# Scaling softmax probabilities on GpSimd in place of ScalarE in a hybrid encoder block

## The chip, the cores and the metric

The kernel runs on one core of a Trainium2 chip. The metric is the device time of one execution in microseconds (us); the median of the runs is compared. The engines of the core are TensorE (PE in the profile; its weight loads are shown apart as PEld), VectorE (DVE), ScalarE (ACT), GpSimd (POOL) and SyncE (SP), which issues nearly all DMAs. The TensorE clock that the throttle grants stands in the profile as a share of full speed.

## The reference

One layer of a bidirectional encoder block, for 1024 positions of width 1024, all in float32. A projection feeds two branches: gated linear attention (GLA) and attention in a window of +-128 positions (SWA). Their outputs are gated and projected, and a SwiGLU feed-forward follows. The change lies in the window attention: 8 query heads in two groups of 4, 2 key-value heads of width 128, blocks of 128 queries against up to three blocks of keys, and a learned sink logit that joins the softmax:

```python
scores = jnp.einsum("bnqhgd,bnkhd->bnhgqk", qb, kc) * (hd ** -0.5)
scores = jnp.where(mask[None, :, None, None], scores, -jnp.inf)
m = jnp.maximum(scores.max(axis=-1, keepdims=True), sink)
p = jnp.exp(scores - m)
denom = p.sum(axis=-1, keepdims=True) + jnp.exp(sink - m)
o = jnp.einsum("bnhgqk,bnkhd->bnqhgd", p / denom, vc)
```

## The kernel before

All products of float32 values are made from two parts: a value is rounded to a high part (on ScalarE, a copy to a reduced float32 format) and the rest is its low part (on VectorE, value minus high part), and three matmuls (line 76: high x high, high x low, low x high) make a product. Line 70 and line 72 do this for weights (wh, wl).

The program goes through the projections and the GLA branch, then from about 575 to 745 us through the window attention, then through the output projections, the gates and the feed-forward.

The window attention works on 16 blocks, 2 groups of heads x 8 blocks of 128 queries. Each block passes through stages in successive slots of a software pipeline (the list `todo`): its raw queries are loaded; a slot later they are normed and rotated (`a_prep`; the small tiles rt, rl and rs of lines 98 to 104 are the inverse norm, and qn the rotated queries); then transposed and split (`a_turn`: PE L923, ACT sqh L926, DVE sql L927); then scored (`a_scores`); two slots later the probabilities are transposed and split (`a_probs`) and multiplied by the values (`a_out`). So in one slot blocks n-2, n, n+1 and n+2 are worked on at once.

The steps of `a_scores` for a block: four heads one after another, three matmuls each into a PSUM buffer ch (line 76), and one VectorE instruction (line 941) that adds the band mask, writes the scores p to SBUF and their largest value mx. When all four are there, VectorE makes nm (the negated maximum, lines 948 to 950) and es (the sink's exponent, line 952); ScalarE exponentiates es (line 953) and the four heads of p (line 956, whose accumulator gives the row sum dn); VectorE adds es to dn (line 958) and takes the reciprocal rd (line 960); then the four heads of p are multiplied by rd (line 962). A row of p is 384 wide, or 256 at the two ends of the sequence.

In `a_probs`, for each of up to three key blocks, TensorE transposes the four heads (line 973) into ch; ScalarE makes the high part ph (line 976), VectorE the low part pl (line 977). In `a_out` TensorE makes three matmuls per key block, in the order ph x vSh, pl x vSh, ph x vSl (vSh and vSl are the parts of the values). ScalarE copies the output to sob (line 987), and four DMAs write it to DRAM. There are four PSUM buffers ch and four mm, and two buffers for p.

TensorE's order is written by hand: in a slot the steps come as a_probs, a_prep, a_scores, a_turn, a_out (with the key steps of the first blocks between), and between them stand matmuls of a dense projection, whose tiles are mm (15 matmuls a slot in most slots, 18 in the last ones). The order of the instructions on the other engines is chosen by a scheduler from its own cost estimates, so an edit of one instruction can reorder others. Each engine takes its instructions strictly in that order.

At the start of the slot in which the scores are over (three slots ahead of the end), `prep_b(0)` begins to load the finished outputs back from DRAM (lo) and to split them (obh on ScalarE, line 1001; obl on VectorE, line 1002) for the output projection. The gates of that projection (gb; VectorE line 1108, ScalarE line 1109) are loaded then too.

Of the kernel before, what the change touches and what calls it, by code (L numbers as in the profile page):

```python
# [11 lines left out]
AF = mybir.ActivationFunctionType  # L12
ALU = mybir.AluOpType
# [17 lines left out]
def body(tc, i, out):  # L31
    nc = tc.nc
    with ExitStack() as root:
# [8 lines left out]
        def nm(s):  # L42
            uid[0] += 1
            return f"{s}_{uid[0]}"
# [4 lines left out]
        def chtile(shape, dt=F32):  # L49
            return psc.tile(list(shape), dt, tag="ch", name=nm("ch"))  # L50
# [27 lines left out]
        def mm3(o, ah, al, bh, bl, start, stop):  # L78
            mm(o, ah, bh, start, False)
            mm(o, ah, bl, False, False)  # L80
            mm(o, al, bh, False, stop)
# [849 lines left out]
        def a_scores(g, n, h):  # L931
            a = att[g, n]
            if h == 0:
                a.p = sw.tile([P, 4, 384], F32, tag="p", name=nm("p"))
                a.mx = sw.tile([P, 4], F32, tag="mx", name=nm("mx"))
            w, p, mx = a.w, a.p, a.mx
            ks = slice(a.b0 * P, (a.b1 + 1) * P)
            mo = (a.b0 - (n - 1)) * P
            s = chtile((P, 384))
            mm3(s[:, :w], a.qh[:, h], a.ql[:, h], kTh[:, g, ks], kTl[:, g, ks], True, True)  # L940
            nc.vector.tensor_tensor_reduce(out=p[:, h, :w], in0=s[:, :w], in1=band[:, mo:mo + w],
                                           op0=ALU.add, op1=ALU.max, scale=1.0, scalar=-1e30,
                                           accum_out=mx[:, h:h + 1])
            if h < 3:
                return
            sk = sink[:, 4 * g:4 * g + 4]
            nm_ = sw.tile([P, 4], F32, tag="nm", name=nm("nm"))
            nc.vector.tensor_tensor(mx, mx, a.rs, op=ALU.mult)
            nc.vector.tensor_tensor(mx, mx, sk, op=ALU.max)
            nc.vector.tensor_scalar(nm_, mx, -1.0, None, op0=ALU.mult)  # L950
            es = sw.tile([P, 4], F32, tag="es", name=nm("es"))
            nc.vector.tensor_tensor(es, sk, mx, op=ALU.subtract)
            nc.scalar.activation(es, es, AF.Exp)
            dn = sw.tile([P, 4], F32, tag="dn", name=nm("dn"))
            for h in range(4):
                nc.scalar.activation(p[:, h, :w], p[:, h, :w], AF.Exp, bias=nm_[:, h:h + 1],  # L956
                                     scale=a.rs[:, h:h + 1], accum_out=dn[:, h:h + 1])
            nc.vector.tensor_tensor(dn, dn, es, op=ALU.add)
            rd = sw.tile([P, 4], F32, tag="rd", name=nm("rd"))
            nc.vector.reciprocal(rd, dn)  # L960
            for h in range(4):
                nc.scalar.activation(p[:, h, :w], p[:, h, :w], AF.Copy, scale=rd[:, h:h + 1])

        def a_probs(g, n, kb):
            a = att[g, n]
# [47 lines left out]
        for n in range(2 * KT):  # L1013
            g, t = divmod(n, KT)
            todo[n + 5].append((a_out, g, t))
            todo[n + 5] += [(a_probs, g, t, kb) for kb in range(3)]
            todo[n + 3] += [(a_scores, g, t, h) for h in range(4)]
            todo[n + 2].append((a_turn, g, t))
            todo[n + 1].append((a_prep, g, t))
            if n < KT:  # L1020
                todo[n + 1].append((k_turn, n))
                todo[n].append((k_prep, n))
                if n:
                    todo[n - 1].append((k_load, n))
            todo[n].append((a_load, g, t))
        order = (a_probs, k_prep, a_prep, a_scores, a_turn, k_turn, a_out, k_load, a_load)
        k_load(0)
        with tc.manual_schedule(engines={mybir.EngineType.PE}):
# [508 lines left out]
```

## Time and profile before

| | |
|---|---|
| median of 3 runs | 1648.97 us (1647.95 to 1650.07) |
| profiled execution | 1649.93 us |
| its span, first to last instruction | 1648.1 us |
| outside the span | 1.8 us |
| mean granted TensorE clock | 0.999 |
| busy: PE, DVE, ACT, POOL | 1628.2, 1249.4, 872.3, 0.2 us |

How to read it: the busy time of an engine is the time in which it executes, so its idle time is the span less that. A row of a timeline has the start (us), the duration (us), the engine, the line of the kernel, the operation, the tiles (out<-in, buffer numbers left out) and the shapes; in brackets at its end stand the idle time of the engine just ahead of it and what ended that. With x4 at its end a row stands for four instructions in a row. A row of the waits has the engine and tile that waited, what it waited for, then the us in total, the times, and the longest. A row of a window has its two ends, its length, the busy time and number of instructions on PE, PEld, DVE, ACT and POOL, the granted clock, the share of the DMA engines' time and GB/s. A row of a group of instructions has its busy time in us, the mean of one in ns, and the idle time ahead of them.

### The profile page before, as it was taken

The numbers are of one execution on the slowest core, as the hardware profiler recorded it, in microseconds if no ns is written. First come the engines' busy times: TensorE is split into PE (matmuls) and PEld (weight loads), VectorE is DVE, ScalarE is ACT, GpSimd is POOL, SyncE is SP. The second block draws the span as 40 slices with busy tenths as digits, with TensorE's granted clock in tenths as the row PEclk, the third lists the DMA queues.
The fourth block names the chain that finished last, engine by engine and source line by source line (L and its number), as shares of the span: only waits on it lengthen the run. The fifth ranks groups of instructions, "written<-read, shape, count | busy, mean of one in ns | idle before, by whom it ended". The sixth has DMA issues, their size and how long they took to land.

```text
span 1648.1 us, 23225 instructions
## 1 busy us (share of the span) xinstructions
PE 1628.2 (99%) x7588; PEld 1346.5 (82%) x7588; DVE 1249.4 (76%) x2559; ACT 872.3 (53%) x1826; POOL 0.2 (0%) x4
## 2 busy tenths in 40 slices
PE   9999999999999999999999999999999999999999
PEld 7888888888888778878888888888888888888887
DVE  8867665589986599857885678887777778779655
ACT  8622224468998688885554557333333333354442
POOL 0000000000000000000000000000000000000000
PEclk9999999999999999999999999999999999999999
DMA  7554334485554633238765554453334443496433
GB/s 235 171 184 147 116 118 138 170 253 173 178 162 128 190 115 97 74 124 280 226 205 171 168 152 148 128 160 109 103 109 155 146 147 128 168 349 192 147 98 120
DMA packets 168010, 262.90 MB, mean 160 GB/s; under 512 B 19325, under 2 KB 52861, under 8 KB 167889
## 3 DMA queue, kind: packets, MB, share of 16 engines
q1 hardware_dynamic: 167888, 261.42, 49.9%
q8 instruction: 60, 0.98, 0.3%
q14 instruction: 62, 0.50, 0.1%
HBM read 187.93 MB, written 73.42 MB: 159 GB/s over the span
## 4 chain that ended last, share of the span: by engine, by line
PE 84%; DVE 8%; ACT 5%; DMA 1%; issue 1%; SPq 0%; ACTq 0%
PE mm L76 23%; PE mm L306 9%; PE mm L308 9%; PE mm L307 9%; PE mm L1350 7%; PE ch L1350 5%; PE ch L76 4%; PE ch L308 4%; PE ch L307 4%; PE ch L306 4%; PE ch L460 3%; PE mm L460 2%; ACT p L956 1%; DVE cs L655 1%; DVE wl L72 1%
## 5 line engine op out<-in xcount | busy, mean ns | idle before, releaser
L298 ACT ACTIVATE wh<-ws 128x512 fp32r<-128x512 f32 x132 | 83.3, 632 | 196.6 <-PE mm L307 104.5
L70 ACT ACTIVATE wh<-wr 128x512 fp32r<-128x512 f32 x202 | 124.9, 626 | 83.3 <-PE mm L76 47.7
L72 DVE TENSOR_TENSOR wl<-wr,wh 128x512 fp32r<-128x512 f32 x202 | 137.2, 684 | 26.3 <-ACT wh L70 26.1
L298 ACT ACTIVATE wh<-wr 128x512 fp32r<-128x512 f32 x69 | 43.6, 632 | 125.0 <-issue 49.9
L299 DVE TENSOR_TENSOR wl<-ws,wh 128x512 fp32r<-128x512 f32 x132 | 90.2, 684 | 22.4 <-ACT wh L298 22.3
L298 ACT ACTIVATE wh<-a 128x512 fp32r<-128x512 f32 x64 | 40.5, 633 | 91.1 <-PE mm L1350 42.6
L76 PE MATMUL mm<-wh,xl 128*128 128x512 f32 x192 | 83.0, 432 | 0.0
L76 PE MATMUL mm<-wh,xh 128*128 128x512 f32 x192 | 79.7, 415 | 0.0
L76 PE MATMUL mm<-wl,xh 128*128 128x512 f32 x192 | 79.6, 414 | 0.0
L299 DVE TENSOR_TENSOR wl<-a,wh 128x512 fp32r<-128x512 f32 x64 | 44.2, 690 | 43.0 <-ACT wh L298 42.6
L1350 PE MATMUL mm<-hh,wh 128*128 128x512 f32 x176 | 68.5, 389 | 0.0
L1350 PE MATMUL mm<-hl,wh 128*128 128x512 f32 x176 | 68.5, 389 | 0.0
L1350 PE MATMUL mm<-hh,wl 128*128 128x512 f32 x176 | 68.5, 389 | 0.0
L76 PE MATMUL mm<-xh,wh 128*128 128x512 f32 x160 | 64.6, 404 | 1.2 <-ACT wh L70 1.2
L76 PE MATMUL mm<-xl,wh 128*128 128x512 f32 x160 | 64.5, 403 | 0.1
L76 PE MATMUL mm<-xh,wl 128*128 128x512 f32 x160 | 59.2, 409 | 0.0
L1320 DVE TENSOR_TENSOR hl<-hr,hh 128x512 fp32r<-128x512 f32 x75 | 51.3, 684 | 3.7 <-ACT hh L1319 3.7
L1350 PE MATMUL ch<-hh,wh 128*128 128x512 f32 x132 | 51.3, 389 | 0.0
L1350 PE MATMUL ch<-hl,wh 128*128 128x512 f32 x132 | 51.3, 389 | 0.0
L1350 PE MATMUL ch<-hh,wl 128*128 128x512 f32 x132 | 51.3, 389 | 0.0
L76 PE MATMUL mm<-oah,wh 128*128 128x512 f32 x128 | 50.2, 392 | 0.0
L76 PE MATMUL mm<-oal,wh 128*128 128x512 f32 x128 | 49.8, 389 | 0.0
(620 smaller groups left out, 5058.6 us busy)
## 6 DMA issues: line engine op xcount, KB each, us to landing
wr<-in_w_fi_dram SPq DMA_DIRECT2D x102, 256.0 KB
wr<-in_w_f_dram SPq DMA_DIRECT2D x80, 256.0 KB
wr<-in_w_t_dram SPq DMA_DIRECT2D x56, 256.0 KB
B<-c SPq DMA_DIRECT2D x44, 256.0 KB
T<-tx SPq DMA_DIRECT2D x44, 256.0 KB
a<-in_w_fo_dram SPq DMA_DIRECT2D x44, 256.0 KB
hr<-T SPq DMA_DIRECT2D x44, 256.0 KB
wr<-in_w_ob_dram SPq DMA_DIRECT2D x32, 256.0 KB
```

Of the source, the lines that this page charges most:

```text
L70: nc.scalar.activation(h, raw, AF.Copy)
L72: nc.vector.tensor_tensor(l, raw, h.bitcast(F32), op=ALU.subtract)
L76: nc.tensor.matmul(o, a, b, start=start, stop=stop)
L298: nc.scalar.activation(h, src, AF.Copy)
L299: nc.vector.tensor_tensor(l, src, h.bitcast(F32), op=ALU.subtract)
L306: nc.tensor.matmul(o, h[:, c], x[kk][0], start=start and kk == 0, stop=False, skip_group_check=True)
L307: nc.tensor.matmul(o, h[:, c], x[kk][1], start=False, stop=False, skip_group_check=True)
L308: nc.tensor.matmul(o, l[:, c], x[kk][0], start=False, stop=kk == nk - 1, skip_group_check=True)
L460: nc.tensor.matmul(ys[m], a[:, c], b, start=f0, stop=f1, skip_group_check=True)
L655: nc.vector.tensor_tensor_scan(csf, mask.rearrange("p c t -> p (c t)"), ef, 0.0, op0=ALU.mult, op1=ALU.add)
L1320: nc.vector.tensor_tensor(l, r, h.bitcast(F32), op=ALU.subtract)
L1350: nc.tensor.matmul(ys[m], a[:, c], b, start=f0, stop=f1, skip_group_check=True)
```

## The change

The four products of p with rd in each block become GpSimd instructions instead of ScalarE activations. The result is the same tile.

```diff
@@ a_scores, line 962
             nc.vector.reciprocal(rd, dn)
             for h in range(4):
-                nc.scalar.activation(p[:, h, :w], p[:, h, :w], AF.Copy, scale=rd[:, h:h + 1])
+                nc.gpsimd.tensor_scalar(p[:, h, :w], p[:, h, :w], rd[:, h:h + 1], None, op0=ALU.mult)
```

TensorE's order is unchanged. GpSimd had only a few memsets at the start. Its rows, before (-) and after (+), first and last of the sixteen groups of four; the numbers behind p and rd are those of the block's buffers:

```order
 L1525 MEMSET const-uint8-127 128x1
-L1532 UNCONDITIONAL_BRANCH x2
+L1532 UNCONDITIONAL_BRANCH
+L962 ISA
+L962 TENSOR_SCALAR p_7097<-p_7097,rd_7136 128x256 x4
+L962 TENSOR_SCALAR p_7209<-p_7209,rd_7248 128x384 x4
```

Sixteen such groups stand there now, one for each block, behind one instruction of another kind (ISA) that waits for nothing.

ScalarE near the end of the window attention: p_9042 is the last block (15), sob_9107 the output of block 13, obh_9128 and obh_9134 the first splits for the output projection, and ph_9179 the first transposed probabilities of block 14.

```order
+L956 ACTIVATE p_9042,dn_9083<-p_9042,nm_9076,rs_8795 128x256
+L953 ACTIVATE es_9080<-es_9080 128x4
+L956 ACTIVATE p_9042,dn_9083<-p_9042,nm_9076,rs_8795 128x256 x3
 L987 COPY sob_9107<-ch_9097 128x512
-L953 ACTIVATE es_9080<-es_9080 128x4
-L956 ACTIVATE p_9042,dn_9083<-p_9042,nm_9076,rs_8795 128x256 x4
 L1001 ACTIVATE obh_9128<-lo_9126 128x512
-L962 ACTIVATE p_9042<-p_9042,rd_9089 128x256 x4
 L1001 ACTIVATE obh_9134<-lo_9132 128x512
 L976 ACTIVATE ph_9179<-ch_9174 128x512
```

The exponentials of block 15 moved ahead of the copy sob, and the four products no longer stand between the two obh. ScalarE in the turn of block 13 (p_8811) shows the same move of the exponentials:

```order
+L956 ACTIVATE p_8811,dn_8844<-p_8811,nm_8837,rs_8533 128x384
+L953 ACTIVATE es_8841<-es_8841 128x4
+L956 ACTIVATE p_8811,dn_8844<-p_8811,nm_8837,rs_8533 128x384 x3
 L987 COPY sob_8878<-ch_8868 128x512
-L953 ACTIVATE es_8841<-es_8841 128x4
-L956 ACTIVATE p_8811,dn_8844<-p_8811,nm_8837,rs_8533 128x384 x4
 L976 ACTIVATE ph_8907<-ch_8902 128x512
 L976 ACTIVATE ph_8917<-ch_8912 128x512
-L962 ACTIVATE p_8811<-p_8811,rd_8850 128x384 x4
 L976 ACTIVATE ph_8928<-ch_8923 128x512
```

Here the third ph no longer stands behind the products. VectorE at the same end of the stage, before:

```order
L952 TENSOR_TENSOR es_9080<-sink,mx_9043 128x4
L1108 TENSOR_TENSOR gb_9370<-gb_9370,rstd 128x512
L1108 TENSOR_TENSOR gb_9412<-gb_9412,rstd 128x512
L958 TENSOR_TENSOR dn_9083<-dn_9083,es_9080 128x4
L960 RECIPROCAL rd_9089<-dn_9083 128x4
L1002 TENSOR_TENSOR obl_9129<-lo_9126,obh_9128 128x512
L1002 TENSOR_TENSOR obl_9135<-lo_9132,obh_9134 128x512
L977 TENSOR_TENSOR pl_9180<-ch_9174,ph_9179 128x512
L977 TENSOR_TENSOR pl_9193<-ch_9187,ph_9192 128x512
L977 TENSOR_TENSOR pl_9207<-ch_9201,ph_9206 128x512
```

And after:

```order
L952 TENSOR_TENSOR es_9080<-sink,mx_9043 128x4
L958 TENSOR_TENSOR dn_9083<-dn_9083,es_9080 128x4
L960 RECIPROCAL rd_9089<-dn_9083 128x4
L1002 TENSOR_TENSOR obl_9129<-lo_9126,obh_9128 128x512
L1002 TENSOR_TENSOR obl_9135<-lo_9132,obh_9134 128x512
L977 TENSOR_TENSOR pl_9180<-ch_9174,ph_9179 128x512
L977 TENSOR_TENSOR pl_9193<-ch_9187,ph_9192 128x512
L977 TENSOR_TENSOR pl_9207<-ch_9201,ph_9206 128x512
L1108 TENSOR_TENSOR gb_9370<-gb_9370,rstd 128x512
L1108 TENSOR_TENSOR gb_9412<-gb_9412,rstd 128x512
```

The two gate products moved behind the three pl of block 14.

In the earlier slots the reordering on VectorE is smaller. One place, block 3 (dn_7499, rd_7505), with the splits of block 2's probabilities around it:

```order
+L958 TENSOR_TENSOR dn_7499<-dn_7499,es_7496 128x4
 L125 TENSOR_TENSOR st_7614<-mm_7200,rstd 128x512
-L958 TENSOR_TENSOR dn_7499<-dn_7499,es_7496 128x4
+L960 RECIPROCAL rd_7505<-dn_7499 128x4
 L977 TENSOR_TENSOR pl_7560<-ch_7554,ph_7559 128x512
-L960 RECIPROCAL rd_7505<-dn_7499 128x4
```

The reciprocal stands one row earlier there, ahead of a split.

## The prediction

> **What bounds the kernel now.** I read the head of the page first, then the busy times by stretch, then the waits and the timeline of the stretch in which line 962 runs. The page:
>
> ```profile
> span 1648.1 us, 23225 instructions
> PE 1628.2 (99%) x7588; PEld 1346.5 (82%) x7588; DVE 1249.4 (76%) x2559; ACT 872.3 (53%) x1826; POOL 0.2 (0%) x4
> ```
>
> TensorE is busy for all but 1648.1 - 1628.2 = 19.9 us. As its order and its instructions stay, the change can move the time by what it does to those gaps and to TensorE's clock. Two stretches, with busy time of PE, PEld, DVE, ACT and POOL, then the granted clock:
>
> ```profile
> 574.00:760.00 186.00, 175.90 (x925) 145.78 (x926) 151.19 (x480) 149.26 (x372) 0.00 (x0) 0.99 0.39 121
> 760.00:1648.00 888.00, 884.47 (x3898) 731.19 (x3896) 677.78 (x1086) 381.14 (x641) 0.00 (x0) 1.00 0.50 162
> ```
>
> The attention stage (574 to 760) holds 186.0 - 175.9 = 10.1 us of the idle time. Behind it TensorE hardly stops, so nothing swallows a microsecond won here, or makes up for a lost one. The waits of the stage (us in total, times, longest), its transfer wait, and the group of line 962:
>
> ```profile
> ACT sob L987 <- PE ch L76: 16.4, 12, 2.6
> PE ch L76 <- DVE mx L941: 3.1, 6, 0.7
> PE ch L923 <- DVE mx L941: 2.0, 2, 1.8
> PE ch L76 <- ACT ph L976: 2.0, 1, 2.0
> PE ch L76 <- DVE rd L960: 1.1, 2, 0.7
> PE ch L76 <- DVE pl L977: 0.9, 1, 0.9
> DVE gb L1108 <- DMA gb<-gb: 2.6, 1, 2.6
> L962 ACT ACTIVATE p<-p,rd 128x384 f32<-128x384 f32 (+1 forms) x64 | 32.4, 581 | 1.5 <-DVE rt L103 0.9 <-DVE rd L960 0.4
> ```
>
> TensorE's rows sum to 9.1 us. None names line 962: the transposes that read its result (L973) wait for nothing. So 32.4 us leave an engine on which TensorE waits by name once, for 2.0 us (ph). The other 7.1 us are waits on VectorE. One loop of the stage shows why, from the timeline:
>
> ```profile
> 698.25 0.59 ACT L987 COPY sob<-ch 128x512 f32<-128x512 f32 x1 [1.79 <-PE ch L76]
> 698.74 0.71 ACT L956 ACTIVATE p<-p,nm,rs 128x384 f32<-128x384 f32 x1
> ...
> 701.75 0.16 DVE L958 TENSOR_TENSOR dn<-dn,es 128x4 f32<-128x4 f32 x1 [2.30 <-ACT p L956]
> 701.94 0.18 DVE L960 RECIPROCAL rd<-dn 128x4 f32<-128x4 f32 x1
> 702.17 0.56 DVE L941 CUSTOM_DVE_ANT_0 p<-ch,band 128x384 f32<-128x384 f32 x1
> 702.22 2.14 ACT L962 ACTIVATE p<-p,rd 128x384 f32<-128x384 f32 x4
> 702.80 0.45 PE L76 MATMUL ch<-kTh,sqh 128*128 128x384 f32 x1 [0.43 <-DVE mx L941]
> ...
> 708.58 0.59 ACT L987 COPY sob<-ch 128x512 f32<-128x512 f32 x1 [1.63 <-PE ch L76]
> ```
>
> ScalarE idles 1.79 us for the output's matmuls, copies it (sob), and only then takes up the exponentials behind it. dn and rd wait for these, and behind them in VectorE's queue the next L941, which holds a PSUM buffer that the next score matmul needs. That matmul's run ends in the next sob: 708.58 - 698.25 = 10.33 us a turn. Line 962 starts beside L941 and lies outside this loop.
>
> **The change part by part.** *The bulk of the 64 products.* Off ScalarE they free 32.4 us that this loop does not use: 0 us. They come back on an idle engine, and the four of a block must be done before the block's first transposes. Three blocks, rd and then these transposes:
>
> ```profile
> 588.59 0.17 DVE L960 RECIPROCAL rd<-dn 128x4 f32<-128x4 f32 x1
> 592.12 0.60 PE L973 MATMUL ch<-ident,p 128*128 128x128 f32 x4
> 596.93 0.17 DVE L960 RECIPROCAL rd<-dn 128x4 f32<-128x4 f32 x1
> 601.29 0.60 PE L973 MATMUL ch<-ident,p 128*128 128x128 f32 x4
> 615.64 0.17 DVE L960 RECIPROCAL rd<-dn 128x4 f32<-128x4 f32 x1
> 622.33 0.60 PE L973 MATMUL ch<-ident,p 128*128 128x128 f32 x4
> ```
>
> That leaves 592.12 - 588.59 - 0.17 = 3.36 us (block 0, 256 wide), 4.19 us (block 1, 384 wide) and 6.52 us; by the same two rows the other thirteen have 4.4 to 8.0 us. So block 1 sets the point: 4.19 / 4 = 1.05 us for one 384-wide product. No row shows GpSimd at such work. Below, nothing can be won (the transposes already wait for nothing); the nearest row is ScalarE's 0.58 us. I take 0.6 to 1.0 us, so 0 us, and keep dearer prices for a rival. [...]
>
> *The end of the stage.* Here line 962 does stand ahead of something urgent:
>
> ```profile
> 727.45 0.17 DVE L950 TENSOR_SCALAR nm<-mx 128x4 f32<-128x4 f32 x1
> 727.99 0.59 ACT L987 COPY sob<-ch 128x512 f32<-128x512 f32 x1 [2.56 <-PE ch L76]
> 728.58 0.59 ACT L956 ACTIVATE p<-p,nm,rs 128x256 f32<-128x256 f32 x1
> 730.25 1.33 DVE L1108 TENSOR_TENSOR gb<-gb,rstd 128x512 f32<-128x512 f32 x2 [2.56 <-DMA gb<-gb]
> 731.22 0.60 PE L973 MATMUL ch<-ident,p 128*128 128x128 f32 x4
> 731.50 0.16 DVE L958 TENSOR_TENSOR dn<-dn,es 128x4 f32<-128x4 f32 x1
> 731.69 0.18 DVE L960 RECIPROCAL rd<-dn 128x4 f32<-128x4 f32 x1
> 731.96 1.71 ACT L962 ACTIVATE p<-p,rd 128x256 f32<-128x256 f32 x4 [0.42 <-DVE rd L960]
> 733.57 0.61 ACT L1001 ACTIVATE obh<-lo 128x512 fp32r<-128x512 f32 x1
> 734.09 1.54 ACT L976 ACTIVATE ph<-ch 128x512 fp32r<-128x512 f32 x3
> 734.72 0.78 PE L76 MATMUL ch<-ph,vSh 128*128 128x512 f32 x1 [1.97 <-ACT ph L976]
> ```
>
> In this order gb waits for its DMA ahead of dn on VectorE, rd comes late, line 962 waits for it and runs 1.71 us, then obh, then the ph that TensorE has needed since 734.72 - 1.97 = 732.75. In the new order the exponentials stand ahead of sob, gb behind the last pl, and line 962 not in the queue. Worked with the same durations: exponentials from nm at 727.62, es (some 0.2) and 4 x 0.59 to 730.2; sob to 730.8; two obh to 732.0; the first ph (its transposes are long done) at 732.6, before TensorE asks. On VectorE the two obl (0.7 each, behind their obh) end at 732.8 and the first pl (0.6) at 733.4, where the second matmul, due about 733.0, waits some 0.45. Of 1.97 + 0.57 (the first wait for ph, then for the first pl: part of the 0.9 row) stay 0.45: -2.0 us, with ends 0 (the lo transfer of the second obh is what is late) and -2.5.
>
> Behind that gap the clock halves:
>
> ```profile
> 735.00:736.00 1.00, 0.93 (x2) 0.44 (x2) 1.00 (x2) 0.97 (x3) 0.00 (x0) 0.50 0.94 336
> 737.00:738.00 1.00, 1.00 (x4) 0.79 (x3) 0.30 (x1) 0.99 (x2) 0.00 (x0) 0.50 0.25 94
> ```
>
> The granted clock is 0.50 from 735 to 738, at both edges a little more, about 3.4 us at half speed, so 1.7 us of work lost. If the gap shrinks to 0.45, I take the whole -1.7 (ends 0 and -1.7). [...] The trace shows the dip right behind the longest wait of the stage, so I go by the trace.
>
> *Block 13.* Its exponentials now stand ahead of sob too. At most the 0.59 of sob leaves that turn of the loop: -0.6 (0 to -0.6). What is late next is L941 itself.
>
> *What GpSimd does to VectorE.* A new neighbour on the same memory may hold up operations there:
>
> ```profile
> 597.59 0.15 DVE L102 TENSOR_TENSOR rt<-rt,rl 128x4 f32<-128x4 f32 x1
> ```
>
> This one reads two tiles in SBUF and stands among the L941 of a block. VectorE is busy 151 of 186 us, and in the slots where TensorE waits for L941 (six times) a delay reaches TensorE at full price. Bounds: 0, and one product's 0.6 us in each of the six, 3.6 us. I take a third, 0.2 each, as most such operations meet no product: +1.2. Everything else is free: GpSimd's first row, an ISA without a wait, has 588 us to run in; the DMA queues carry the same transfers.
>
> Sum against the profiled execution (1649.93 us, span 1648.1 and 1.8 around it): 0 - 2.0 - 1.7 - 0.6 + 1.2 = -3.1, so 1646.8. The profiled run is 0.96 above the median of the runs, 1648.97, so the median after is 1645.9.
>
> **The rivals.** *Slow products (slower).* If one 384-wide product takes over 1.05 us, block 1's transposes are late, then the rest as the slack of each is used up. At 1.8 us a block needs 7.2 us: late by 3.0 at block 1, some 1.4 at block 0 and mostly 0.2 to 2.5 in ten others, about +13 together, 1659. It decides the sign from about 1.5 us on. Against it: 0.58 us on ScalarE for plain arithmetic, and slack of 6 us and more in most blocks.
>
> *VectorE held up all through.* If each block costs TensorE 0.2 us (16 x 0.2 = 3.2 in place of 1.2), and the clock dips once where it did not before, behind the longest L923 wait of 1.8 us, which would grow (+1.7), the sum is +0.6, about 1649.6. For it: VectorE ends TensorE's waits. [...] No row of this profile has POOL at work. Against it: L941, L977 and sql read one operand from PSUM.
>
> *The end stays as it is.* The lo transfer or another wait takes the place of line 962 ahead of ph: -3.7 falls away, +0.6, 1649.6. Against it: the second obh began right after line 962, without a wait of its own.
>
> *A larger gain.* A freer ScalarE lets dn and rd come sooner in more turns than block 13's, since rd stands earlier in VectorE's new order in places. Half of the 6.2 us of L941 and rd waits go: -3.1 more, 1642.8.
>
> That the change does nothing of what it says is excluded: the new order has all sixteen groups of four on POOL.
>
> **How the numbers follow.** Forecast 0.52, slow products 0.13, VectorE held up 0.18, the end as it is 0.07, larger gain 0.10. The measurement tells about 0.2% (3.3 us) from no change, so faster means below 1645.7. The forecast lies at that edge: half of it (0.26), with the larger gain and a little of the rest, 0.38. Slower (above 1652.3) is the slow products and a tail of the held-up VectorE: 0.15. Same: 0.47. The range goes from 1641.5 (just below the larger gain; all terms of the forecast at their good ends give -4.8, 1644.2) to 1652.5, which takes in the second and third rival and +3.6 for the collisions, and leaves out most of the slow products. The likeliest case alone has 1644.2 to 1648.3 (the gap's 2.0 us not won, or the clock's 1.7).
>
> **What would show it.** POOL rows of L962 below 1.05 us start to start and no wait `PE ch L973 <- POOL` show the bulk right. At 732 to 739 the gap ahead of ch<-ph,vSh should be under 0.6 us, with the clock at 1.00. VectorE's L102, L103 and L72 should keep their durations, except beside a POOL row. TensorE's waits on L941 should stay between 5 and 8 us. I am wrong if the transposes wait for POOL, if the clock still falls to 0.50 at 735, or if the stage's idle time grows.

## The result and the profile after

The kernel with the products on GpSimd takes 1645.59 us in the median of 14 runs (1644.88 to 1646.95), against 1649.74 (1647.34 to 1651.37) for 14 runs of the kernel before beside it: a ratio of 0.9977, with a 95% interval of 0.9969 to 0.9984. That is 4.1 us less by the medians, 3.8 by the ratio. Three experiments below had one or two executions far above their others, which their medians and comparisons leave out; the trace of one_tensor_tensor is such an execution (clock 0.654 throughout), so only the durations on the other engines are read from it, no waits of TensorE.

The head of the page after, the attention stage by stretch (columns as before), and the group of line 962:

```profile
span 1643.8 us, 23281 instructions
PE 1626.0 (99%) x7588; PEld 1346.0 (82%) x7588; DVE 1251.4 (76%) x2559; ACT 842.6 (51%) x1762; POOL 76.0 (5%) x68
```

```profile
574.00:760.00 186.00, 176.96 (x936) 147.56 (x935) 155.55 (x484) 121.43 (x310) 75.82 (x64) 1.00 0.40 125
```

```profile
L962 POOL TENSOR_SCALAR p<-p,rd 128x384 f32<-128x384 f32 (+1 forms) x64 | 75.8, 1202 | 657.1 <-DMA qr<-sq 587.2
```

ScalarE lost 149 - 121 = 28 us of work in the stage, GpSimd took on 76, and TensorE was busy for 1 us more of it. The products cost 1.20 us each on GpSimd where ScalarE took 0.58. TensorE's waits in the stage now:

```profile
PE ch L76 <- DVE mx L941: 2.6, 5, 0.5
PE ch L923 <- DVE mx L941: 1.9, 1, 1.9
PE ch L76 <- DVE pl L977: 1.8, 3, 1.0
PE ch L973 <- POOL p L962: 0.9, 2, 0.6
```

The wait for ph (2.0) is gone, those on L941 have hardly changed (5.1 before, 4.5 now), and one row is new: transposes that wait for GpSimd.

**Where the time went.** TensorE runs the same 7588 instructions in the same order in both kernels. So the start of one and the same instruction in two traces can be subtracted, and what the difference gains or loses between two instructions is what the stretch between them gained or lost. Every number of the next table is made in this way, against the first profile of before; the stretches are named by the times of before. Minus is time won.

| trace | first 20 us | 590 to 603 | 603 to 722 | 722 to 725 | 725 to 740 |
|---|---|---|---|---|---|
| the whole change | -1.24 | +1.48 | +0.22 | -0.92 | -3.77 |
| only_block15 | -0.67 | 0.00 | +0.02 | 0.00 | -3.03 |
| all_but_block15 | -1.41 | +1.49 | +0.27 | -0.92 | +0.01 |
| act_blocks01 | -1.14 | +0.01 | +0.32 | -0.92 | -4.09 |
| no_scale | -1.03 | +1.03 | -0.67 | -0.93 | -4.08 |
| blocks14_15 | -1.24 | +0.01 | -0.01 | -0.58 | -2.69 |
| blocks14_15_gate_off | -0.63 | +1.59 | -0.01 | -0.59 | -2.76 |
| blocks12_15 | -0.55 | +0.02 | +0.07 | -0.93 | -4.08 |
| gate_off_vector | -0.71 | 0.00 | -0.01 | 0.00 | -0.88 |
| double_pool_load | -0.15 | -0.01 | +4.35 | -0.93 | +8.77 |
| products_on_vector | -1.07 | +2.78 | +11.70 | -0.92 | +0.17 |
| before_again | -1.11 | +1.59 | +0.08 | 0.00 | +0.30 |

The first column is chance: every trace is ahead of the first profile of before by then, the same kernel taken again by 1.11 us. The other columns of the whole change sum to 1.48 + 0.22 - 0.92 - 3.77 = -2.99. Between 20 and 590 lie another -0.17, and behind 740 the difference stays at -4.4 to the end.

Half clock is part of these numbers, and the traces differ in it. The first profile of before has one stretch of it, at the end of the stage, so a trace without one there gains some 1.7 us in the last column by that alone; only all_but_block15, double_pool_load, products_on_vector and before_again have one there too. Between 590 and 603, no_scale, blocks14_15_gate_off, products_on_vector and before_again have one that the first profile has not, and products_on_vector has another between 603 and 722.

The end of the stage after, to be held against the rows of before:

```profile
725.94 0.60 ACT L956 ACTIVATE p<-p,nm,rs 128x256 f32<-128x256 f32 x1 [2.71 <-DVE es L952]
728.71 0.18 DVE L960 RECIPROCAL rd<-dn 128x4 f32<-128x4 f32 x1
729.08 4.23 POOL L962 TENSOR_SCALAR p<-p,rd 128x256 f32<-128x256 f32 x4 [3.47 <-ACT sob L987]
730.85 1.55 ACT L976 ACTIVATE ph<-ch 128x512 fp32r<-128x512 f32 x3
731.62 1.88 DVE L977 TENSOR_TENSOR pl<-ch,ph 128x512 fp32r<-128x512 f32 x3
731.96 0.40 PE L76 MATMUL ch<-ph,vSh 128*128 128x512 f32 x1
732.36 0.50 PE L76 MATMUL ch<-pl,vSh 128*128 128x512 f32 x1
733.42 1.28 DVE L1108 TENSOR_TENSOR gb<-gb,rstd 128x512 f32<-128x512 f32 x2
```

The matmul on ph starts without a wait in brackets, 2.76 us earlier than before; the products run beside it on GpSimd, and gb comes last. The clock that stood at 0.50 here:

```profile
735.00:736.00 1.00, 1.00 (x8) 0.85 (x7) 0.79 (x2) 1.00 (x3) 0.00 (x0) 1.00 0.72 268
```

And the start of the stage, where the new row of waits comes from (blocks 0 and 1):

```profile
587.17 0.17 DVE L960 RECIPROCAL rd<-dn 128x4 f32<-128x4 f32 x1
587.59 3.90 POOL L962 TENSOR_SCALAR p<-p,rd 128x256 f32<-128x256 f32 x4 [587.17 <-DMA qr<-sq]
591.55 0.33 PE L973 MATMUL ch<-ident,p 128*128 128x128 f32 x1 [0.35 <-POOL p L962]
596.08 0.17 DVE L960 RECIPROCAL rd<-dn 128x4 f32<-128x4 f32 x1
596.42 5.16 POOL L962 TENSOR_SCALAR p<-p,rd 128x384 f32<-128x384 f32 x4 [4.93 <-ACT vSh L894]
601.64 0.33 PE L973 MATMUL ch<-ident,p 128*128 128x128 f32 x1 [0.58 <-POOL p L962]
```

The four products of a 384-wide block take 4.9 us (5.2 here), more than the 4.19 us that block 1 has. The fourth head's transpose waits. The two waits make 0.93 of the 1.48 us lost there; the rest is not told apart.

The stretch at 722, where 0.92 us were won, before:

```profile
721.32 2.13 ACT L962 ACTIVATE p<-p,rd 128x384 f32<-128x384 f32 x4
722.07 0.42 DVE L941 CUSTOM_DVE_ANT_0 p<-ch,band 128x256 f32<-128x256 f32 x1 [0.84 <-PE ch L76]
723.21 0.42 DVE L941 CUSTOM_DVE_ANT_0 p<-ch,band 128x256 f32<-128x256 f32 x1 [0.71 <-PE ch L76]
723.37 1.54 ACT L976 ACTIVATE ph<-ch 128x512 fp32r<-128x512 f32 x3
```

and after:

```profile
720.46 1.74 ACT L976 ACTIVATE ph<-ch 128x512 fp32r<-128x512 f32 x3
722.89 0.41 DVE L941 CUSTOM_DVE_ANT_0 p<-ch,band 128x256 f32<-128x256 f32 x1
```

Before, block 14's products stood ahead of the three ph of block 13. Three of the four buffers ch wait for these ph and their pl, so the scores of block 15 had one buffer left and went back and forth between TensorE and VectorE (0.84, 0.71). After, the ph come 2.9 us earlier, the buffers are free, and the scores run through.

### The profile page after: what moved, and what is told of

The parts are those of the page before. It is cut to its first block, busy times and chain, and to the rows that moved or that the text cites. A ratio compares the mean times of both kernels' runs of the same rounds, so it can differ in the third digit from the quotient of the medians.

```text
span 1643.8 us, 23281 instructions
## 1 busy us (share of the span) xinstructions
PE 1626.0 (99%) x7588; PEld 1346.0 (82%) x7588; DVE 1251.4 (76%) x2559; ACT 842.6 (51%) x1762; POOL 76.0 (5%) x68
## 4 chain that ended last, share of the span: by engine, by line
PE 84%; DVE 9%; ACT 4%; DMA 2%; issue 1%; POOL 1%; SPq 0%; ACTq 0%; DVEq 0%
PE mm L76 23%; PE mm L306 9%; PE mm L308 9%; PE mm L307 9%; PE mm L1350 7%; PE ch L1350 5%; PE ch L76 4%; PE ch L306 4%; PE ch L308 4%; PE ch L307 4%; PE ch L460 3%; PE mm L460 2%; ACT p L956 1%; DVE wl L72 1%; DVE cs L655 1%
## 5 line engine op out<-in xcount | busy, mean ns | idle before, releaser
L962 POOL TENSOR_SCALAR p<-p,rd 128x384 f32<-128x384 f32 (+1 forms) x64 | 75.8, 1202 | 657.1 <-DMA qr<-sq 587.2
```

What stands on the lines that cost most here:

```text
L962: nc.gpsimd.tensor_scalar(p[:, h, :w], p[:, h, :w], rd[:, h:h + 1], None, op0=ALU.mult)
```

## The experiments

Theory A said that the gain sits in ScalarE's queue at the end of the stage. Its rivals: B, relief of ScalarE in all slots; C, the new places of gb and of the exponentials. A cost of GpSimd's own (late products, VectorE held up) was open besides. "Before" is the kernel before on the same chip.

**only_block15**

```diff
-nc.scalar.activation(p[:, h, :w], p[:, h, :w], AF.Copy, scale=rd[:, h:h + 1])
+nc.gpsimd.tensor_scalar(p[:, h, :w], p[:, h, :w], rd[:, h:h + 1], None, op0=ALU.mult) if g * KT + n == 15 else nc.scalar.activation(p[:, h, :w], p[:, h, :w], AF.Copy, scale=rd[:, h:h + 1])
```

> Only block 15's products go to GpSimd; the other fifteen blocks stay on ScalarE. Against the kernel before. Theory A (the gain sits in ScalarE's queue at the end of the stage, where the last block's products stood ahead of obh and ph): -2.5 to -3.7 us; up to 720 us the two traces run alike, then the gap ahead of ch<-ph,vSh falls from 1.97 to under 0.6 us and the clock stays at 1.00. Rival B (the relief of ScalarE in all slots): one sixteenth of it, 0 to -0.4 us. Rival C (the gain hangs on gb's new place on VectorE and on the earlier exponentials, neither of which moves here): within 0.5 us of before, with the clock dip still there.

Measured: 1646.13 us, ratio 0.9978 (0.9969 to 0.9987), 3.3 us by the medians. From 590 to 725 the traces are alike to 0.02 us. At the end gb still stands ahead of dn, and the exponentials behind sob:

```profile
729.37 1.33 DVE L1108 TENSOR_TENSOR gb<-gb,rstd 128x512 f32<-128x512 f32 x2 [2.56 <-DMA gb<-gb]
731.72 0.49 PE L76 MATMUL ch<-ph,vSh 128*128 128x512 f32 x1
732.83 0.50 PE L76 MATMUL ch<-pl,vSh 128*128 128x512 f32 x1 [0.62 <-DVE pl L977]
```

The wait for ph is gone with the one block's four products. A wait of 0.62 us for pl is left, since obl and pl stand behind gb. B falls: four of the 64 products bring most of the gain. C is not needed for it.

**all_but_block15**

```diff
-... if g * KT + n == 15 else ...
+... if g * KT + n < 15 else ...
```

> Blocks 0 to 14 go to GpSimd, block 15 stays on ScalarE, where its products now stand ahead of both obh. Against the kernel before. Theory A: the gap of about 2 us ahead of ch<-ph,vSh and the half clock come back, so that only the late products of blocks 0 and 1 (+1.3) and block 13's exponentials (-0.9) are left: 0 to +1 us. Rival B (relief of ScalarE in all slots): about -3 us, as the whole change. Rival C (earlier exponentials are the gain): -2 us or better, since they stand ahead of sob here too.

Measured: 1647.34 us, 0.9988 (0.9979 to 0.9997), 2.1 us by the medians. That is outside A's numbers, and within reach of B's and C's. Its end:

```profile
728.73 1.71 ACT L962 ACTIVATE p<-p,rd 128x256 f32<-128x256 f32 x4
731.17 1.29 DVE L1108 TENSOR_TENSOR gb<-gb,rstd 128x512 f32<-128x512 f32 x2 [2.54 <-DMA gb<-gb]
732.01 0.50 PE L76 MATMUL ch<-ph,vSh 128*128 128x512 f32 x1
734.32 0.67 PE L76 MATMUL ch<-pl,vSh 128*128 128x512 f32 x1 [1.81 <-DVE pl L977]
```

The products are on ScalarE, ahead of both obh, and yet ph is in time, because the exponentials stand ahead of sob in this order and everything behind them is 3 us earlier. But gb, waiting for its load, stands ahead of obl and pl, and TensorE waits 1.81 us for pl. So A as I had put it is too simple: two queues are late at the end, ScalarE's (ph) and VectorE's (pl, behind gb), and the change relieves both. In this profile the clock fell behind the new wait (0.50 from 735 to 736), and the end won nothing (+0.01). In 6 of its 11 runs the mean clock was 1.000, in 12 of 81 runs of before, and the profiled execution was the slowest of the 11; so the median is better than the trace.

**act_blocks01**

```diff
-... if g * KT + n == 15 else ...
+... if g * KT + n > 1 else ...
```

> Blocks 0 and 1 stay on ScalarE, 2 to 15 go to GpSimd. Against the kernel before. Theory A with a cost of 1.2 to 1.3 us for GpSimd's lateness at blocks 0 and 1 (the transposes waited for POOL at 591.5, and behind it the clock or VectorE): -4.3 us in the trace's attention stage, 1.2 better than the whole change. If the 1.3 us lost at the start of the stage comes from the scheduler's order of VectorE there or from VectorE held up by GpSimd later: -3 us, as the whole change.

Measured: 1644.04 us, 0.9969 (0.9957 to 0.9981), 5.4 us by the medians. The 1.48 us between 590 and 603 are gone to 0.01. They belong to the products of blocks 0 and 1 on GpSimd, as the other stretches changed by 0.3 us at most.

**no_scale**

```diff
-                nc.gpsimd.tensor_scalar(p[:, h, :w], p[:, h, :w], rd[:, h:h + 1], None, op0=ALU.mult)
+                pass
```

> The products with the reciprocal are left out on every block, so the probabilities stay unnormalised. Against the kernel before. This is the bound of what any placing of line 962 can give. Theory A without any cost from GpSimd at work: the same as with blocks 0 and 1 on ScalarE, -4.2 to -4.6 us. If GpSimd holds up VectorE through blocks 2 to 15 by shared access to SBUF: better than that by over 1 us, -5.5 or more. If ScalarE's relief mattered in the bulk: -6 or more.

This kernel leaves the products out. Measured: 1643.04 us, 0.9962 (0.9949 to 0.9974), 6.4 us by the medians: 1.0 below act_blocks01, with intervals that overlap. From 603 to 722 it won 0.67 where act_blocks01 lost 0.32. So the products on GpSimd cost the slots between some 1.0 us against no products at all; how much of it is VectorE held up and how much another order is not told apart. (Between 590 and 603 its profile had half clock, 0.50 at 592.)

**blocks14_15**

```diff
-... if g * KT + n == 15 else ...
+... if g * KT + n >= 14 else ...
```

> Only the products of blocks 14 and 15 go to GpSimd. Against the kernel before. Theory A2 (two places only: block 14's products stood ahead of three ph at 721 to 725 us, worth 0.9; block 15's ahead of obh and ph at the end, worth 2 and a chance of half clock): in the trace -0.9 by 726 us, and -2.5 to -4.2 in all, with a wait for pl of 0.6 to 1.5 us left at the end, because gb's load still stands ahead of obl and pl on VectorE. Rival (the 0.9 near 725 us comes from relief that adds up over all slots): nothing there, -3.3 us in all as with block 15 alone.

Measured: 1645.36 us, 0.9976 (0.9967 to 0.9985), 4.05 us by the medians. It won 0.58 at 722 to 725, where only_block15 won nothing, so that gain belongs to block 14's products. The other 0.34 of the 0.92 came only in the kernels that move more blocks. At the end, with the first gb ahead of dn and the second ahead of obl, the wait for pl was 1.07 us:

```profile
728.26 0.69 DVE L1108 TENSOR_TENSOR gb<-gb,rstd 128x512 f32<-128x512 f32 x1 [3.06 <-DMA gb<-gb]
729.15 0.66 DVE L1108 TENSOR_TENSOR gb<-gb,rstd 128x512 f32<-128x512 f32 x1
731.87 0.50 PE L76 MATMUL ch<-pl,vSh 128*128 128x512 f32 x1 [1.07 <-DVE pl L977]
```

What is won ahead of the end is partly given back there, as gb's load does not come sooner.

**gate_off_vector**

```diff
-                nc.vector.tensor_tensor(g, g, rstd[:, s * HT:(s + 1) * HT], op=ALU.mult)
+                (nc.gpsimd if nme in ("gb0", "gb1") and s == 0 else nc.vector).tensor_tensor(g, g, rstd[:, s * HT:(s + 1) * HT], op=ALU.mult)
```

> The products with the reciprocal stay on ScalarE as before; the first two gate products gb (line 1108), which wait for their load, go from VectorE to GpSimd. Against the kernel before. Theory A2: dn and rd then wait for the exponentials alone, which stand behind sob and end at 731.0, so rd is only 0.5 us earlier and the gap ahead of ch<-ph,vSh falls from 1.97 to about 1.5 us: -0.3 to -1 us, the clock dip stays. Rival C (gb's wait is the cause of the late end): -2 to -3.7 us, gap under 0.6 us, no dip.

Measured: 1650.49 us, 1.0006 (0.9998 to 1.0015): nothing won. The profile is the one execution of the 11 with a mean clock of 1.000; its -0.88 in the table is the half clock that did not come, against a wait for ph that grew from 1.97 to 2.33 us. Neither expectation was met; the trace shows why:

```profile
730.21 2.52 POOL L1108 TENSOR_TENSOR gb<-gb,rstd 128x512 f32<-128x512 f32 x2 [729.77 <-DMA b<-sob]
730.55 0.96 DVE L958 TENSOR_TENSOR dn<-dn,es 128x4 f32<-128x4 f32 x1 [3.35 <-ACT p L956]
731.65 1.63 DVE L1002 TENSOR_TENSOR obl<-lo,obh 128x512 fp32r<-128x512 f32 x1
734.58 0.50 PE L76 MATMUL ch<-ph,vSh 128*128 128x512 f32 x1 [2.33 <-ACT ph L976]
```

dn, which takes 0.16 us elsewhere, took 0.96 and ended at 731.51, 0.04 us behind the end of the first of the two gb on GpSimd (730.21 + 1.26 = 731.47); obl took 1.63 in place of 0.69 and ended at 731.65 + 1.63 = 733.28, 0.55 us behind the end of the second gb (732.73). Both read two tiles in SBUF, and so does a gb. In these rows neither ended before the gb beside it. So rd came no earlier, and C (gb's wait alone) can't be judged by this run.

**blocks14_15_gate_off**: both edits together.

> Products of blocks 14 and 15 and the first two gate products on GpSimd. Against the kernel before. Theory A2: all of 0.9, 2.0 to 2.5 and the clock, nothing lost at blocks 0 and 1: -4.5 to -5.5 us; in the trace no wait of over 0.6 us between 715 and 740 us. If GpSimd's work in the other slots had won something of its own, this is worse than the kernel with blocks 0 and 1 on ScalarE (-5.4 us) by over 1 us.

Measured: 1646.30 us, 0.9981 (0.9972 to 0.9990), 3.1 us by the medians: no better than blocks14_15, against the expectation. The wait for pl at the end was still 1.01 us: the first gb on GpSimd stood beside obl, and the two obl took 2.36 us in place of 1.31. Its +1.59 near 590 is half clock. And 0.94 us go between 740 and 745:

```profile
737.81 0.63 ACT L1109 ACTIVATE gb<-gb 128x512 f32<-128x512 f32 x1 [3.19 <-POOL gb L1108]
```

GpSimd takes the second gb only behind block 15's products, ScalarE waits 3.19 us for it, and the ph of block 15 stand behind that in ScalarE's queue.

**double_pool_load**: act_blocks01 with more work on GpSimd.

```diff
+            for h in range(4 if g * KT + n > 1 else 0):
+                nc.gpsimd.tensor_scalar(dm[:, :w], band[:, :w], rd[:, h:h + 1], None, op0=ALU.mult)
```

> As the kernel with blocks 0 and 1 on ScalarE, but behind the four products of each of blocks 2 to 15 GpSimd multiplies the band mask by rd four more times into a tile that nobody reads, so that it works nearly 10 us of each slot of 10.3. Against the kernel before. If GpSimd's work in itself holds VectorE up: 1 us or more is lost against the kernel with blocks 0 and 1 on ScalarE (-5.4 us), so -4.4 us or worse, and VectorE's small operations on two SBUF tiles (L102, L103, L917) take longer. If it does not: within 0.5 us of -5.4, unless the next block's products queue behind the extra ones and the transposes wait for POOL, which the waits would show.

Measured: 1660.85 us, 1.0068 (1.0056 to 1.0081), 11.4 us slower than before. The tile dm is read by nobody. The kernel lost 4.35 us from 603 to 722, and 8.77 at the end. The loss at the end is one wait of TensorE for ph, with 10.2 us of half clock from 741.3 on:

```profile
745.61 1.15 ACT L1004 ACTIVATE obh<-lo 128x512 fp32r<-128x512 f32 x2 [8.41 <-POOL dm L965]
747.30 0.80 PE L76 MATMUL ch<-ph,vSh 128*128 128x512 f32 x1 [8.82 <-ACT ph L979]
```

The two obh stand ahead of that ph on ScalarE and began when the last extra product ended. So these 8.77 us come from what waited for the extra instructions, and tell nothing of VectorE. In the slots before, both kinds of cost show: transposes waited three times for POOL (1.9 us in all), as products queued behind the extra ones, and the waits on L941 and pl make 5.9 us in place of act_blocks01's 4.4. Single small operations of VectorE took three times as long as their 0.15:

```profile
646.36 0.43 DVE L959 TENSOR_TENSOR dn<-dn,es 128x4 f32<-128x4 f32 x1 [1.58 <-ACT p L957]
652.55 0.47 DVE L103 SCALAR_TENSOR_TENSOR rt<-rt,rl 128x4 f32<-128x4 f32 x1
```

How much of the longer waits on VectorE is such hold-up and how much another order is not told apart. With the single load of the change the same is there, smaller: L102 from 155 to 203 ns in the mean in the stretch 603 to 724, before and after (L948 from 153 to 185):

```profile
L102 DVE TENSOR_TENSOR rt<-rt,rl 128x4 f32<-128x4 f32 x11 | 1.7, 155 | 0.3 <-ACT rl L99 0.3
```

```profile
L102 DVE TENSOR_TENSOR rt<-rt,rl 128x4 f32<-128x4 f32 x11 | 2.2, 203 | 0.0
```

**before_again**: the kernel before, unchanged.

> The kernel before, unchanged, as a control: the ratio is 1.000 within its interval. Its trace shows whether the 1.0 to 1.4 us by which the first 9 us of the profiled execution of before were longer than in the other traces belong to the kernel (then they are there again) or to that execution (then they are gone, and this trace's span is about 1 us shorter); and whether the half clock behind the end of the attention stage comes in each execution.

Measured: 1650.5 us, 1.0008 (0.9998 to 1.0017): no difference shown. The medians are 1.3 us apart all the same, as six of its ten executions had a mean clock of 0.998 and only four of the 22 beside it; so one microsecond between two medians is little. The first 20 us were 1.11 us shorter than in the first profile, so that loss belonged to the execution. The clock fell at the end again, and also behind the wait at 590, where the first profile had it at 1.00:

```profile
589.00:590.00 1.00, 1.00 (x7) 0.82 (x5) 0.83 (x4) 0.97 (x2) 0.00 (x0) 0.50 0.76 238
736.00:737.00 1.00, 1.00 (x3) 0.81 (x4) 1.00 (x3) 0.98 (x2) 0.00 (x0) 0.50 0.88 231
```

**blocks12_15**

```diff
-... if g * KT + n == 15 else ...
+... if g * KT + n >= 12 else ...
```

> Products of blocks 12 to 15 on GpSimd. On VectorE gb stands behind the three pl in this order, on ScalarE the exponentials ahead of sob, as in the whole change. Against the kernel before. Theory A2: all of the two places' gain and nothing of the cost at blocks 0 and 1 or in the slots between: in the trace -0.9 at 725 us, and -3.5 to -3.8 more (with the half clock of that profile) by 740 us, so a median 1 to 1.7 us below the whole change's ratio, -5 to -6 us. If most of the kernel with blocks 0 and 1 on ScalarE (-5.4) came from the other slots: -4 us, as blocks 14 and 15 alone.

Measured: 1644.24 us, 0.9969 (0.9957 to 0.9981), 5.0 us by the medians. Four blocks bring all that act_blocks01 brings with fourteen: -0.93 and -4.08 in the last two columns. Against blocks14_15 the end is 1.39 better: here gb stands behind pl. This and act_blocks01 are the best of the kernels that compute the whole, about 1.3 us below the whole change (0.9969 each against 0.9977; the intervals overlap).

**one_tensor_tensor**

```diff
-            for h in range(4):
-                nc.gpsimd.tensor_scalar(p[:, h, :w], p[:, h, :w], rd[:, h:h + 1], None, op0=ALU.mult)
+            nc.gpsimd.tensor_tensor(p[:, :, :w], p[:, :, :w], rd[:, :, None].to_broadcast([P, 4, w]), op=ALU.mult)
```

> All sixteen blocks on GpSimd, but one two-input instruction for the four heads of a block (p times rd, rd repeated along the row) instead of four with rd as a scalar operand. From the gate products that GpSimd took (1.26 us for 512 elements a row) an estimate of 3 to 3.8 us a block of 1536 elements instead of 4.92. Against the kernel before. If the loss at blocks 0 and 1 is lateness: no wait of the transposes for POOL at 601 us (slack 4.19), and 0.5 to 1.3 us better than the whole change, -4.6 to -5.4. If two-input work on GpSimd holds VectorE up for its whole length, as the gate products held dn and obl: small VectorE operations of 0.15 us grow to 1 us and more in many slots, and the kernel is slower than the whole change.

Measured: 1652.28 us, 1.0018 (1.0009 to 1.0027), 3.1 us slower than before, though GpSimd needed only 2.75 us a block. So shorter products on GpSimd made the kernel slower, as expected if two-input work there holds VectorE up; the clock was below 1.000 in all its 11 runs. The hold-up itself stands in the trace:

```profile
836.50 2.75 POOL L961 TENSOR_TENSOR p<-p,rd 128x1536 f32<-128x1536 f32 x1 [9.73 <-ACT rl L99]
836.85 2.41 DVE L102 TENSOR_TENSOR rt<-rt,rl 128x4 f32<-128x4 f32 x1
```

This operation, 0.16 us long elsewhere, ended at 839.26, 0.01 us after the product (839.25). Five small operations of VectorE were held in this way and took 0.56 to 2.41 us; one obl took 1.95. How much of this reached TensorE is not shown.

**products_on_vector**

```diff
-                nc.gpsimd.tensor_scalar(p[:, h, :w], p[:, h, :w], rd[:, h:h + 1], None, op0=ALU.mult)
+                nc.vector.tensor_scalar(p[:, h, :w], p[:, h, :w], rd[:, h:h + 1], None, op0=ALU.mult)
```

> All sixteen blocks' products on VectorE. Against the kernel before. VectorE is busy 151 of the stage's 186 us and TensorE waits for L941 on it; 64 products of 0.25 to 0.42 us are 16 to 27 us more. Theory (VectorE's part of the loop sets the length of a turn): a good share of it reaches TensorE, +3 to +15 us, although the end of the stage is relieved as on GpSimd. If VectorE's idle time in the slots takes them in: -1 to -4 us.

Measured: 1661.73 us, 1.0076 (1.0064 to 1.0089), 12.5 us slower. The groups and the waits of its stage:

```profile
L962 DVE TENSOR_SCALAR p<-p,rd 128x384 f32<-128x384 f32 (+1 forms) x64 | 21.4, 398 | 0.2
```

```profile
PE ch L76 <- DVE pl L977: 11.2, 11, 2.4
```

VectorE is the engine that does these products fastest (0.40 us in the mean, against 0.58 on ScalarE in before and 1.20 on GpSimd in after; the 0.25 to 0.42 of the expectation were an estimate of mine), and the wrong place: TensorE lost 11.70 us between 603 and 722. Some 1.7 of that is half clock (634 to 637.4); the largest part are waits for pl, which stands behind the products.

## Why the prediction was right, step by step

The forecast was -3.1 us; the traces give -2.99 without the chance of the first 20 us, the medians -4.1; where the further 1.1 us lie, these traces do not settle. The sum is right partly because errors cancel, so that it came out this close is in part luck. One of the signs of being wrong that the prediction named did come: the transposes waited for POOL. Its other two did not: the clock did not fall at 735, and the stage's idle time went from 10.1 us to 9.0.

**The bulk (0 us)** was wrong at its edge. I had named the point, 1.05 us a product, and taken 0.6 to 1.0, an estimate upward from ScalarE's 0.58; it is 1.23 (a block's four take 4.92 us). The row at the end of this document has 0.92 us for the shortest, 256 wide, and 1.25 in the median, 384 wide, about twice ScalarE's 0.49 and 0.60 in before. So blocks 0 and 1 were late and 1.48 us were lost, which act_blocks01 takes away. In that the rival of slow products came true in its first step, and only there, since the slack of the other blocks held. That the 32 us of freed ScalarE are worth nothing in the loop held: 603 to 722 shows +0.22, and blocks12_15, with three quarters of the products still on ScalarE, gains as much as act_blocks01.

**The end (-2.0) and the clock (-1.7)** were right in size: the first matmul on ph won 2.13 us (-0.63 to -2.76), and the matmuls behind it up to 740 won 1.64 more, in which the half clock and the matmul on pl lie together: -3.77 for a forecast of -3.7. One piece of the -2.0 was misread: the 0.57 us for pl is not part of the 0.9 row, whose single wait lies at 626.6. Before, the matmul on pl started 0.84 us behind the one on ph, partly at half clock, and no wait stood there. Without the 0.57 the same working gives -1.5. As to cause, I had put the three moves (products out, exponentials ahead, gb behind pl) into one sum. The experiments separate them: the products alone win most (only_block15); with exponentials ahead the products can even stay, but then gb's place decides (all_but_block15).

The clock's part was a matter of chance, which the forecast had not said. Of 81 executions of before in the experiments' comparisons 12 have a mean clock of 1.000 (mean 1647.7 us), 50 of 0.999 (1649.4), 18 of 0.998 (1651.2) and one of 0.997: a thousandth costs 1.7 us, as I had worked out for one spell. After the change 11 of 14 have 1.000, and the other three, with 1645.4 to 1645.7 us, were no longer than these. So one and the same kernel has such a spell in some executions and not in others. In the profiles half clock followed waits of 1.97 us (before), of 1.9 and 2.2 (before_again) and of 1.81 (all_but_block15), and the change takes away the longest wait at one of the two places where the two profiles of before show it.

The traces also show something of the chance. The half clock of before lasted from 734.77 to 738.18, 3.41 us, and its clock fell again at 1649.54, behind the last instruction. The two stretches of before_again began at 588.62 and 735.39, by the clocks of 0.81 at 588 and 0.60 at 738 in its windows: 146.77 us apart, 43 steps of 3.413 us. From 738.18 to 1649.54 it is 267 such steps. So the changes of the clock in each of these two traces fit a grid of 3.413 us, and double_pool_load's 10.2 us of half clock are three steps of it. The step ahead of the half clock in before, its step with the next most idle time between 100 and 1600 us and the one behind that, then two steps of gate_off_vector:

```profile
731.35:734.77 3.42, 1.45 (x10) 0.93 (x8) 1.63 (x5) 3.00 (x8) 0.00 (x0) 1.00 0.75 229
587.99:591.41 3.42, 1.61 (x10) 1.26 (x10) 3.40 (x14) 2.62 (x7) 0.00 (x0) 1.00 0.82 270
591.41:594.82 3.41, 3.41 (x21) 2.96 (x20) 3.28 (x12) 2.43 (x9) 0.00 (x0) 1.00 0.34 105
730.42:733.83 3.41, 1.83 (x11) 1.18 (x9) 2.69 (x3) 2.63 (x8) 2.31 (x2) 1.00 0.57 180
733.83:737.24 3.41, 2.31 (x9) 1.72 (x10) 3.04 (x5) 2.87 (x6) 0.00 (x0) 1.00 0.81 269
```

In before, 3.42 - 1.45 = 1.97 us of one step were idle, and half clock followed; of the other, 3.42 - 1.61 = 1.81 us, and the clock stayed at 1.00. In gate_off_vector a longer wait, 2.33 us, lies across the border between its two steps, which have 1.58 and 1.10 us idle, and the clock stayed at 1.00; where the border lies is an estimate, as that stage has no half clock to mark it. That a wait of 2 us costs its 1.7 us more or not by where it falls on the grid agrees with these rows, but no run tested it alone.

**Block 13 (-0.6)** failed. In its turn nothing changed; 0.92 us were won in the next, by another mechanism that I had in the order before me ("the third ph no longer stands behind the products") and priced at nothing: block 14's products ahead of block 13's ph, which held three buffers. Block 14's products alone make 0.58 of it (blocks14_15).

**VectorE held up (+1.2)** was not measured alone. Against before, 603 to 722 shows +0.22; against the kernel without products it is 0.9 (0.22 + 0.67), in which the held-up VectorE and another order lie together. The hold-up is there: beside two-input work on GpSimd a small operation took up to 0.96 us (gate_off_vector) and 2.41 us (one_tensor_tensor) in place of 0.16, and ended within 0.04 us of GpSimd's instruction. Beside the change's own products it is shorter: of VectorE's small operations in the trace after the longest took 0.33 to 0.47 us, beside products of 1.25.

**The rivals.** Slow products came at blocks 0 and 1 alone; the held-up VectorE did not bring its +0.6; the end did change; "a larger gain" came to less than a third of its size (-0.9 of its -3.1), and in another place. In the likeliest case's range, the upper end of 1648.3 is not what its words give: 1645.9 + 2.0 is 1647.9.

## What to carry to other kernels

Ask of an engine not how full it is but what stands behind the instruction that leaves its queue: four of the 64 products held up something urgent at the end, four others a little earlier, and the rest were free where they were. Then put the work on the idle engine only where its slack covers that engine's slower price; here 4 blocks on GpSimd were as good as 14 and, by the traces, better than 16. And look at the whole order after an edit, since a load that waits in the other engine's queue (gb) can take over the place just cleared.

## What the runs showed of the hardware

The products on GpSimd, from the view by tile of the kernel after (shortest, median and longest in ns; 16 of the 64 are 256 wide, the others 384):

```profile
L962 POOL TENSOR_SCALAR p<-p,rd x64: 922/1247/1740, 587.6 to 732.4; 128x384 f32<-128x384 f32 x48, 128x256 f32<-128x256 f32 x16
```

A multiply by a scalar operand took 0.92 us for 256 elements a row and 1.25 for 384; ScalarE took 0.49 and 0.60 for the same in before, VectorE 0.34 and 0.41 in products_on_vector (shortest and median of the same view). Beside a two-input product on GpSimd, an operation of VectorE that reads two tiles in SBUF took 0.96 us in place of 0.16 (dn in gate_off_vector) and 2.41 in place of 0.16 (rt in one_tensor_tensor), and ended 0.04 and 0.01 us behind it. And behind a wait of TensorE of 1.97 us the clock stood at 0.50 for 3.41 us in before (734.77 to 738.18), an estimate of 1.7 us more; behind one of 2.33 us in gate_off_vector it stayed at 1.00. Of 81 executions of before 69 had a mean clock below 1.000, of 14 after the change three.
